# Splitting every gate and up piece of the short expert queues, with ScalarE evicting their up and the last turn inside the products before it

## The chip, the cores and the metric

The kernel runs on one core of a Trainium2 chip. The metric is the device time of one execution in microseconds. The core has five engines with a queue each, which meet in semaphores: TensorE (PE in the rows, its weight loads PEld), VectorE (DVE), ScalarE (ACT), GpSimd (POOL) and SyncE (SP), which issues the transfers from HBM.

## What is computed

A decoder trunk of two layers on 256 tokens of 1024 channels in float32. Each layer has a token mixer and then a channel mixer: in layer 0 a dense SwiGLU, in layer 1 a top-2-of-8 expert SwiGLU with 3584 inner channels. The change touches the expert part alone:

```python
def swiglu(h, wg, wu, wd):
    return (jax.nn.silu(h @ wg) * (h @ wu)) @ wd

def moe_swiglu(h2, router, wg, wu, wd):       # h2: 256 x 1024
    logits = jnp.matmul(h2, router, preferred_element_type=jnp.float32)
    top_logit, top_e = lax.top_k(logits, TOP_K)        # 2 of 8
    top_w = jax.nn.softmax(top_logit, axis=-1)
    ...
    # every token goes through its two experts; the results are added by weight
    yb = lax.map(expert_block, ...)                    # swiglu(xb, wg[e], wu[e], wd[e])
    return jnp.zeros_like(h2).at[tok_buf].add(yb * w_buf[:, None], mode='drop')
```

## The kernel before

From about 608 us on the kernel runs eight queues of tokens, one for each expert. Queues 0 to 3 are long (up to 128 tokens), queues 4 to 7 short (`SHORT = 64`); which expert stands in which queue is settled at run time by the number of its tokens. Each queue goes through its expert's 3584 inner channels in chunks of 512 (`CH`), two chunks in a step where possible: `steps` lists (queue, first channel, number m of chunks). A short queue has four steps, three with m = 2 and one with m = 1. After a start with two long steps, short and long steps take turns; the last two steps are short.

A step computes the gate product, then the up product (8 row blocks of 128 rows each, 512 columns a chunk), and then `down(*prev, ...)`: the down product of the step before. Weights come as raw tiles of 2 MB each and are used in pieces of 128 x 1024. float32 is computed in parts: `split` makes of a piece a high part `wh` (ScalarE, L121) and a low part `wl` (VectorE, L124). For a long queue the tokens are split too, and a product of 512 columns is three matmuls (L133 to L135). For a short queue the 64 tokens' high and low parts stand side by side as 128 columns of one operand (`xa` for gate and up, `ax` for down), and a product is two matmuls, with `wh` (L904) and `wl` (L905). Some pieces of short queues are not split: `piece(view, whole)` returns the raw view, and `products` multiplies it as float32 with an unsplit copy of the 64 tokens (`xw`, `aw`; L900). In the profile each such product is two matmul instructions. Whole are one gate piece of each short step (p = 1), one up piece of each short step with m = 2, and one of four down pieces.

`take` keeps as many pieces ready as there are buffers (`len(pieces)`, five pairs of wh and wl), so the splits of the next pieces stand in ScalarE's and VectorE's queues ahead of what the program does after taking a piece. `keep_order` fixes the order on PE, DVE and ACT as the code records it.

A short step's gate and up results are evicted from PSUM to SBUF: the gate as it is by ScalarE (L1257), the up by VectorE (L1261). The `turn` of a step happens during the next step's gate pieces: for a short queue TensorE multiplies gate and up rows with `fold` (L917), which turns them and adds the two halves, ScalarE takes Silu (L918), VectorE multiplies (L919), and both split the result into `ax` (L128, L129). For a long queue it is four transposes a half (L928), then L128 and L129 into `ax` and `al`. `dispatch` gathers the tokens of a queue (L828 and what follows), and `combine` brings a queue's result back to the tokens (L948 to L955); these are generators that `advance` moves a stage further at fixed pieces. The last step has no next step: behind the loop stand `settle()`, then its `turn`, and then its four down pieces with two products each.

Of the kernel before, what the change touches and what calls it, by code (L numbers as in the profile page):

```python
# [10 lines left out]
F32 = mybir.dt.float32  # L11
F32R = mybir.dt.float32r
# [3 lines left out]
AF = mybir.ActivationFunctionType  # L16
# [6 lines left out]
DB = D // 128  # L23
# [10 lines left out]
NLONG, SHORT, LEAD = 3, 64, 2  # L34
# [25 lines left out]
def trunk_kernel(ctx: ExitStack, tc: tile.TileContext, x, positions, norm1_g, w_in, q_norm_g, w_uq,  # L60
# [15 lines left out]
    consts = pool("consts", "left")  # L76
# [686 lines left out]
    def moe(l, norm, lgT):  # L763
        i = l // 2
        mp = pool("moe", "left")
# [54 lines left out]
        def is_short(r):  # L820
            return r > NLONG
# [9 lines left out]
        def dispatch(r):  # L831


            sh = is_short(r)
            if sh:
                xa = norm_pool.tile([128, DB, 128], F32R, name="xa", tag="hlo0")
                xw = mp.tile([128, 4, SHORT], F32, name="xw", tag="xw")
            else:
                xgh, xgl = (consts.tile([128, DB, 128], F32R, name="xg", tag=f"xT{k}") for k in range(2))
            io = iota2 if sh else iota  # L840
            P = mp.tile([128, 2, 128], BF16, name="P", tag="P", bufs=2)
            C = norm_pool.tile([128, 2, 128], F32, name="C", tag="nsq", bufs=2)
            for t in range(2):
                V.tensor_scalar(P[:, t], io, pos_r[:, t, r:r + 1], None, op0=OP.is_equal)
                V.tensor_scalar(C[:, t], io, pos_r[:, t, r:r + 1], wsel_r[:, t, r:r + 1], op0=OP.is_equal, op1=OP.mult)
            yield
            for j0 in range(0, DB, 4):
                pg = bank()
                gather(pg, j0, P)
                v = pg.rearrange("p (j s) -> p j s", j=4)  # L850
                js = slice(j0, j0 + 4)
                if sh:
                    if j0 == 0:
                        A.activation(xw, v[:, :, :SHORT], AF.Copy)
                    A.activation(xa[:, js, :SHORT], v[:, :, :SHORT], AF.Copy)
                    V.tensor_sub(xa[:, js, SHORT:], v[:, :, SHORT:], f32(xa[:, js, :SHORT]))
                else:
                    split_act(xgh[:, js], xgl[:, js], v)
            yield
            xg[r] = (xa, xw) if sh else (xgh, xgl)  # L860
            back[r] = places(C, sh)

        xg, back, expert = {}, {}, {}
# [9 lines left out]
        def wide(w_, r, f0, n):  # L873

            for h in range(n):
                w = raw_tile().rearrange("p (a b) -> p a b", a=DB // n)
                SP.dma_start(w, weights(w_, r, GU, FE, h * 512, D // n, f0, n * CH))
                a = 2 // n
                for p in range(4):
                    yield piece(w[:, p * a:(p + 1) * a], is_short(r) and h == 0 and p == 1 and (n == 2 or w_ is moe_w_gate))  # L880

        def deep(r, f0, n, by_block=False):

# [8 lines left out]
        def piece(view, whole):  # L892

            return (view,) if whole else split(view)

        def products(o, l, k, r, a, c, start, stop):


            if len(r) == 1:
                PE.matmul(o[:SHORT], l[1][:, k], r[0][:, a, c], start=start, stop=stop)  # L900
            elif l[0].shape[2] == l[1].shape[2]:
                mm3(o, (l[0][:, k], l[1][:, k]), (r[0][:, a, c], r[1][:, a, c]), start, stop)
            else:
                PE.matmul(o, l[0][:, k], r[0][:, a, c], start=start, stop=False)  # L904
                PE.matmul(o, l[0][:, k], r[1][:, a, c], start=False, stop=stop)  # L905

        def turn(r, s, h, acts, P=None):


            pt = bank()  # L910
            js = slice(4 * h, 4 * h + 4)
            if is_short(r):
                ax, aw = acts
                p4 = pt.rearrange("p (k b q) -> p k b q", k=2, b=4)
                for k in range(2):
                    for b in range(4):
                        PE.matmul(p4[:, k, b], s[k][:, (4 * h + b) * 128:(4 * h + b + 1) * 128], fold, start=True, stop=True)  # L917
                A.activation(aw[:, js], p4[:, 0], AF.Silu)  # L918
                V.tensor_mul(aw[:, js], aw[:, js], p4[:, 1])  # L919
                split_act(ax[:, js, :SHORT], ax[:, js, SHORT:], aw[:, js])  # L920
                return
            for b in range(4):
                c = slice(b * 128, (b + 1) * 128)
                if P is not None:
                    for t in range(2):
                        PE.matmul(pt[:, c], s[t][:, c], P[:, t], start=t == 0, stop=t == 1)
                else:
                    PE.transpose(pt[:, c], s[:, (4 * h + b) * 128:(4 * h + b + 1) * 128], ident)  # L928
            split_act(acts[0][:, js], acts[1][:, js], pt.rearrange("p (b q) -> p b q", b=4))
# [34 lines left out]
        def advance(tag="u", always=False):  # L964
            if behind and (always or met[0] - behind[0][1] >= len(pieces)):
                g = behind.pop(0)[0]
                aux[0] = tag
                if next(g, "end") != "end":
                    behind.insert(0, (g, met[0]))
                aux[0] = "u"  # L970
# [206 lines left out]
        def acts_of(r):  # L1177
            one = norm_pool.tile([128, DB, 128], F32R, name="ax", tag="hlo1")
            if is_short(r):
                return one, mp.tile([128, DB, SHORT], F32, name="aw", tag="al")  # L1180
            return one, mp.tile([128, DB, 128], F32R, name="al", tag="al")
# [28 lines left out]

        y = {}

        def down(r, f0, m, acts, banks_at):
            sh = is_short(r)
            if f0 == 0:
                if sh in pending:
                    settle()
                y[sh] = [bank(f"y{int(sh)}") for _ in range(2)]
            for p in range(4 * m):
                pc = take()  # L1220
                for n in range(2):
                    products(y[sh][n], acts, p, pc, 0, slice(n * 512, (n + 1) * 512), f0 == 0 and p == 0,
                             f0 + m * CH == FE and p == 4 * m - 1)
                if p in banks_at:
                    advance(banks_at[p])
            if f0 + m * CH == FE:
                pending.add(sh)
                begin(combine(y[sh], *back[r], sh))
# [3 lines left out]
        for r, f0, m in steps[1:]:  # L1232
            sh = is_short(r)
            while r not in back:
                advance(always=True)
            x = xg[r]
            acts = acts_of(prev[0])
            pg = [bank("g") for _ in range(m)]
            for w in range(2):
                if w:  # L1240
                    pu = [bank() for _ in range(m)]
                    u = rows_tile(1) if sh else None
                for p in range(4 * m):
                    pc = take()
                    for a in range(2 // m):
                        for n in range(m):
                            k = p if m == 2 else 2 * p + a
                            products((pu if w else pg)[n], x, k, pc, a, slice(n * CH, (n + 1) * CH), k == 0, k == DB - 1)
                    t = p - 2 * (m - 1)
                    if w == 0 and 0 <= t < prev[2]:  # L1250
                        turn(prev[0], last[0], t, acts, last[1])
                    elif w == 1 and m == 2 and p == 5:
                        advance("g")
                if w == 0:
                    s = rows_tile(0)
                    for n in range(m):
                        A.activation(s[:, n * CH:(n + 1) * CH], pg[n], AF.Copy if sh else AF.Silu)  # L1257
            for n in range(m):
                c = slice(n * CH, (n + 1) * CH)
                if sh:  # L1260
                    V.tensor_copy(u[:, c], pu[n])  # L1261
                else:
                    V.tensor_mul(s[:, c], s[:, c], pu[n])
            if f0 + m * CH == FE:
                after = r + 1 if r not in (NLONG, NE - 1) else None
                if after:
                    begin(dispatch(after))
            down(*prev, acts, {1: "g", 4: "u"} if m == 1 else {2: "g"} if prev[2] == 1 else {3: "g", 4: "u"})
            prev, last = (r, f0, m), ((s, u) if sh else s, None)

        settle()
        r, f0, m = prev
        acts = acts_of(r)
        turn(r, last[0], 0, acts)
        pcs = [take() for _ in range(4)]
        for n in range(2):
            for b, pc in enumerate(pcs):
# [56 lines left out]
```

## Time and profile before

| | |
|---|---|
| median of 3 runs | 1522.5 us (1522.24 to 1522.84) |
| the profiled execution | 1522.75 us, its span 1521.0 us |
| PE busy | 1487.3 us (98%) |
| PEld busy | 1229.0 us (81%) |
| DVE busy | 1266.6 us (83%) |
| ACT busy | 1017.9 us (67%) |
| POOL busy | 110.4 us (7%) |
| moved by the DMA queues | 439.69 MB, 289 GB/s over the span |

The profile is of one execution. A matmul is drawn from its start to a modelled end, and the next one starts before that end, so the pace of TensorE is read from one start to the next and not from lengths. Merged rows of a timeline (x11) give the first start and the time to the end of the last. "idle before <-releaser" is the time in which the engine stood, and whose semaphore ended it. PEclk is the granted clock of TensorE: 1.00 is 2.4 GHz, 0.50 is 1.2 GHz.

### The profile page before, as it was taken

How to read it: one execution, taken by the hardware profiler on the slowest of the kernel's cores; microseconds unless marked ns; L12 is line 12 of the kernel's file. 1: busy time of each engine (PE TensorE's matmuls, PEld its weight loads, DVE VectorE, ACT ScalarE, POOL GpSimd, SP SyncE). 2: the span in 40 equal slices, each digit the busy share in tenths (PEclk: the TensorE clock that was granted, in tenths of full speed). 3: DMA queues.
4: the chain of work that ended last, by engine and by line, in shares of the span. 5: the costliest groups of instructions: out<-in, count | busy, mean ns of one | idle time of the engine just before them, and what ended most of it. 6: DMA issues, size and time to landing. Idle time of an engine off the chain costs nothing.

```text
span 1521.0 us, 22641 instructions
## 1 busy us (share of the span) xinstructions
PE 1487.3 (98%) x8624; PEld 1229.0 (81%) x8624; DVE 1266.6 (83%) x1787; ACT 1017.9 (67%) x1319; POOL 110.4 (7%) x133
## 2 busy tenths in 40 slices
PE   6999999999999999999999999999999999999997
PEld 5899999999889988768677786777776777777764
DVE  6987876667887888988888998899898889898985
ACT  4596454444487466777776877686777677677773
POOL 5211400002211120000000000000000000000000
PEclk8999999999999999999999999999999999999998
DMA  7338645442336838999999999999999999999990
GB/s 229 112 111 330 224 151 202 148 130 96 115 108 250 304 125 313 381 362 406 358 390 359 351 389 368 374 396 370 346 394 356 387 385 371 350 395 348 405 345 29
DMA packets 139700, 439.69 MB, mean 289 GB/s; under 512 B 5934, under 2 KB 12180, under 8 KB 139588
## 3 DMA queue, kind: packets, MB, share of 16 engines
q1 hardware_dynamic: 139284, 437.58, 76.2%
q8 instruction: 69, 1.13, 0.3%
q0 software_dynamic: 272, 0.62, 0.2%
q14 instruction: 43, 0.35, 0.1%
q10 hardware_dynamic: 32, 0.01, 0.0%
HBM read 437.15 MB, written 1.05 MB: 288 GB/s over the span
## 4 chain that ended last, share of the span: by engine, by line
PE 90%; DVE 6%; ACT 1%; POOL 1%; issue 1%; DMA 1%; SPq 0%; DVEq 0%; ACTq 0%; POOLq 0%
PE bk L133 19%; PE bk L134 19%; PE bk L135 19%; PE bk L904 9%; PE bk L905 8%; PE bk L900 6%; PE bk L917 3%; DVE wl L124 2%; PE bk L828 1%; PE bk L928 1%; POOL nacc L307 1%; PE bk L517 1%; PE bk L540 1%; DMA raw<-in_w_in_dram 1%; PE bk L954 0%
## 5 line engine op out<-in xcount | busy, mean ns | idle before, releaser
L124 DVE TENSOR_TENSOR wl<-raw,wh 128x1024 fp32r<-128x1024 f32 x757 | 896.0, 1227 | 103.9 <-ACT wh L121 100.6
L121 ACT ACTIVATE wh<-raw 128x1024 fp32r<-128x1024 f32 x773 | 789.4, 1054 | 273.7 <-PE bk L134 141.5
L133 PE MATMUL bk<-hh,wh 128*128 128x256 f32 x800 | 233.0, 292 | 5.3 <-ACT hh L299 5.2
L134 PE MATMUL bk<-hlo,wh 128*128 128x256 f32 x800 | 228.9, 286 | 2.1 <-DVE hlo L300 2.1
L135 PE MATMUL bk<-hh,wl 128*128 128x256 f32 x800 | 227.7, 285 | 0.3 <-DVE wl L124 0.3
L133 PE MATMUL bk<-wh,xg 128*128 128x512 f32 x432 | 173.4, 401 | 0.0
L135 PE MATMUL bk<-wh,xg 128*128 128x512 f32 x432 | 170.7, 395 | 0.0
L134 PE MATMUL bk<-wl,xg 128*128 128x512 f32 x432 | 170.6, 395 | 0.0
L133 PEld LDWEIGHTS bk<-hh,wh 128*128 128x128 f32 x800 | 154.6, 194 | 7.5 <-ACT hh L299 5.5
L904 PE MATMUL bk<-wh,xa 128*128 128x512 f32 x392 | 158.6, 405 | 0.0
L134 PEld LDWEIGHTS bk<-hlo,wh 128*128 128x128 f32 x800 | 154.7, 193 | 4.1 <-DVE hlo L300 2.5
L135 PEld LDWEIGHTS bk<-hh,wl 128*128 128x128 f32 x800 | 154.4, 193 | 0.8 <-DVE wl L124 0.7
L905 PE MATMUL bk<-wl,xa 128*128 128x512 f32 x392 | 154.0, 393 | 0.0
L904 PEld LDWEIGHTS bk<-wh,xa 128*128 128x128 f32 x392 | 73.6, 188 | 34.0 <-ACT wh L121 13.0
L135 PEld LDWEIGHTS bk<-wh,xg 128*128 128x128 f32 x432 | 81.1, 188 | 19.5
L134 PEld LDWEIGHTS bk<-wl,xg 128*128 128x128 f32 x432 | 81.3, 188 | 18.1
L133 PEld LDWEIGHTS bk<-wh,xg 128*128 128x128 f32 x432 | 81.3, 188 | 18.1
L134 PE MATMUL bk<-wl,ax 128*128 128x512 f32 x224 | 88.9, 397 | 0.0
L133 PE MATMUL bk<-wh,ax 128*128 128x512 f32 x224 | 88.8, 397 | 0.0
L135 PE MATMUL bk<-wh,al 128*128 128x512 f32 x224 | 88.1, 393 | 0.0
L905 PEld LDWEIGHTS bk<-wl,xa 128*128 128x128 f32 x392 | 73.7, 188 | 14.8 <-DVE wl L124 0.2
L904 PE MATMUL bk<-wh,ax 128*128 128x512 f32 x170 | 71.4, 420 | 1.8 <-DVE ax L129 1.8
(351 smaller groups left out, 2263.4 us busy)
## 6 DMA issues: line engine op xcount, KB each, us to landing
raw<-in_moe_w_gate_dram SPq DMA_DIRECT2D x56, 2048.0 KB, 9.7
raw<-in_moe_w_up_dram SPq DMA_DIRECT2D x56, 2048.0 KB, 9.5
raw<-in_moe_w_down_dram SPq DMA_DIRECT2D x55, 2048.0 KB, 10.8
raw<-in_w_in_dram SPq DMA_DIRECT2D x12, 2048.0 KB, 7.7
raw<-in_ffn_w_gate_dram SPq DMA_DIRECT2D x5, 2048.0 KB, 9.1
raw<-in_ffn_w_up_dram SPq DMA_DIRECT2D x5, 2048.0 KB
raw<-in_ffn_w_down_dram SPq DMA_DIRECT2D x5, 2048.0 KB, 8.0
raw<-in_w_o_dram SPq DMA_DIRECT2D x4, 2048.0 KB
```

The source lines that it names most:

```text
L121: A.activation(hv, view, AF.Copy)
L124: eng.tensor_sub(lv, view, f32(hv))
L133: PE.matmul(o, l[0], r[0], start=start, stop=False, **kw)
L134: PE.matmul(o, l[0], r[1], start=False, stop=False, **kw)
L135: PE.matmul(o, l[1], r[0], start=False, stop=stop, **kw)
L307: G.tensor_add(self.acc, self.acc, sq)
L517: PE.matmul(ps[:, i], qT[:QD, h0 + i, t * 128:(t + 1) * 128], kT[:QD, h0 + i, :nk], start=True, stop=True)
L540: PE.matmul(po[:, i * VD:(i + 1) * VD], pTs[:, i * (t + 1) + kb], vt[:, kb, h0 + i], start=kb == 0, stop=kb == t)
L900: PE.matmul(o[:SHORT], l[1][:, k], r[0][:, a, c], start=start, stop=stop)
L904: PE.matmul(o, l[0][:, k], r[0][:, a, c], start=start, stop=False)
L905: PE.matmul(o, l[0][:, k], r[1][:, a, c], start=False, stop=stop)
L917: PE.matmul(p4[:, k, b], s[k][:, (4 * h + b) * 128:(4 * h + b + 1) * 128], fold, start=True, stop=True)
```

## The change

Every gate and up piece goes through `split`; only down pieces can be whole. `xw` is gone, and a short queue's tokens are the tuple `(xa,)`; `products` tells the kinds apart by that. The up of a short step is evicted by ScalarE (`A.activation(..., AF.Copy)`) instead of VectorE. The last step's `turn` is handed to the last `down` of the loop as `then`, which calls it after the products of the last piece but one; for this the operands of the last down products get places of their own (`ends`), in the memory of `xa` and of a long queue's tokens, which are free by then.

```diff
@@ dispatch
             if sh:
                 xa = norm_pool.tile([128, DB, 128], F32R, name="xa", tag="hlo0")
-                xw = mp.tile([128, 4, SHORT], F32, name="xw", tag="xw")
@@
                 if sh:
-                    if j0 == 0:
-                        A.activation(xw, v[:, :, :SHORT], AF.Copy)
                     A.activation(xa[:, js, :SHORT], v[:, :, :SHORT], AF.Copy)
@@
-            xg[r] = (xa, xw) if sh else (xgh, xgl)
+            xg[r] = (xa,) if sh else (xgh, xgl)
@@ wide
-                    yield piece(w[:, p * a:(p + 1) * a], is_short(r) and h == 0 and p == 1 and (n == 2 or w_ is moe_w_gate))
+                    yield split(w[:, p * a:(p + 1) * a])
@@ products
-            elif l[0].shape[2] == l[1].shape[2]:
+            elif len(l) == 2 and l[1].shape[2] == 128:
@@ down
-        def down(r, f0, m, acts, banks_at):
+        def down(r, f0, m, acts, banks_at, then=None):
@@
                 if p in banks_at:
                     advance(banks_at[p])
+                if then and p == 4 * m - 2:
+                    then()
@@ the loop over steps
                 if sh:
-                    V.tensor_copy(u[:, c], pu[n])
+                    A.activation(u[:, c], pu[n], AF.Copy)
@@
-            down(*prev, acts, {1: "g", 4: "u"} if m == 1 else {2: "g"} if prev[2] == 1 else {3: "g", 4: "u"})
+            then = None
+            if (r, f0, m) == steps[-1]:
+                ends = (norm_pool.tile([128, DB, 128], F32R, name="ax", tag="hlo0"),
+                        consts.tile([128, DB, SHORT], F32, name="aw", tag="xT0"))
+
+                def then():
+                    turn(r, (s, u), 0, ends)
+
+            down(*prev, acts, {1: "g", 4: "u"} if m == 1 else {2: "g"} if prev[2] == 1 else {3: "g", 4: "u"}, then)
@@ behind the loop
         settle()
         r, f0, m = prev
-        acts = acts_of(r)
-        turn(r, last[0], 0, acts)
+        acts = ends
         pcs = [take() for _ in range(4)]
```

The first place is VectorE in a short step of two chunks in the middle of the stage. `wl` is a split, `al` the second half of a long queue's turn, `s` the eviction of up (its tile shares a name with the gate's), `aw` the product in the next, short turn. The order before:

```order
L124 TENSOR_TENSOR wl<-raw,wh 128x1024 x9
L129 TENSOR_TENSOR al<-bk,ax 128x512
L124 TENSOR_TENSOR wl<-raw,wh 128x1024
L129 TENSOR_TENSOR al<-bk,ax 128x512
L124 TENSOR_TENSOR wl<-raw,wh 128x1024 x11
L1261 COPY s<-bk 128x512 x2
L124 TENSOR_TENSOR wl<-raw,wh 128x1024 x9
L919 TENSOR_TENSOR aw<-aw,bk 128x256
```

The same place in the changed kernel, whose line numbers are three lower here:

```order
L124 TENSOR_TENSOR wl<-raw,wh 128x1024 x10
L129 TENSOR_TENSOR al<-bk,ax 128x512
L124 TENSOR_TENSOR wl<-raw,wh 128x1024
L129 TENSOR_TENSOR al<-bk,ax 128x512
L124 TENSOR_TENSOR wl<-raw,wh 128x1024 x21
L916 TENSOR_TENSOR aw<-aw,bk 128x256
```

One split more stands ahead of the turn and one more behind it, and the two evictions between the splits are gone.

The second place is VectorE at the end of the program. `yl` and `xk` belong to the combines (`xk` is the sum over tokens), `aw` and `ax` to the last turn. Before:

```order
L955 TENSOR_TENSOR xk<-xk,bk 128x512 x2
L949 SCALAR_TENSOR_TENSOR yl<-bk,wp,yh 128x512
L124 TENSOR_TENSOR wl<-raw,wh 128x1024 x6
L955 TENSOR_TENSOR xk<-xk,bk 128x512 x2
L919 TENSOR_TENSOR aw<-aw,bk 128x256
L129 TENSOR_TENSOR ax<-aw,ax 128x4x64
L949 SCALAR_TENSOR_TENSOR yl<-bk,wp,yh 128x512
```

In the changed kernel:

```order
L952 TENSOR_TENSOR xk<-xk,bk 128x512 x2
L946 SCALAR_TENSOR_TENSOR yl<-bk,wp,yh 128x512
L124 TENSOR_TENSOR wl<-raw,wh 128x1024 x5
L916 TENSOR_TENSOR aw<-aw,bk 128x256
L129 TENSOR_TENSOR ax<-aw,ax 128x4x64
L124 TENSOR_TENSOR wl<-raw,wh 128x1024
L952 TENSOR_TENSOR xk<-xk,bk 128x512 x2
```

The last turn's two operations moved ahead of the last split and of the additions of the combine before. On TensorE the turn's eight products (16 matmul instructions) now stand ahead of the last piece of the down before it and ahead of that combine's four matmuls.

## Rows read from the trace of the kernel before

**Rows 1.** Stretches: busy us (count) by engine, PEclk, DMA share, GB/s.

```profile
600.00:1500.00 900.00, 898.59 (x4107) 668.58 (x4106) 800.00 (x819) 666.47 (x754) 0.00 (x0) 1.00 0.95 365
1400.00:1450.00 50.00, 50.00 (x221) 36.81 (x220) 44.23 (x44) 36.92 (x43) 0.00 (x0) 1.00 1.01 390
```

**Rows 2.** Waits, 600 to 1500 us: us in total, times, longest.

```profile
ACT wh L121 <- PE bk L135: 65.0, 188, 1.3
...
PEld bk L134 <- DVE wl L124: 1.3, 3, 0.4
...
PEld bk L905 <- DVE wl L124: 0.7, 2, 0.5
```

**Rows 3.** Timeline of PE around a whole piece: start us, us, operation.

```profile
1162.53 0.40 PE L905 MATMUL bk<-wl,xa 128*128 128x512 f32 x1
1162.86 1.93 PE L900 MATMUL bk<-raw,xw 128*64 128x512 f32 x4
...
1165.05 0.39 PE L905 MATMUL bk<-wl,xa 128*128 128x512 f32 x1
```

**Rows 4.** Groups by line and shape: busy us, mean ns | idle before.

```profile
L124 DVE TENSOR_TENSOR wl<-raw,wh 128x1024 fp32r<-128x1024 f32 x753 | 892.6, 1229 | 103.9 <-ACT wh L121 100.6
L121 ACT ACTIVATE wh<-raw 128x1024 fp32r<-128x1024 f32 x769 | 786.9, 1057 | 269.9 <-PE bk L134 139.3 <-PE bk L135 72.9 <-PE bk L904 35.8
...
L900 PE MATMUL bk<-raw,xw 128*64 128x512 f32 x112 | 54.1, 605 | 0.0
...
L1257 ACT ACTIVATE s<-bk 128x512 f32<-128x512 f32 x55 | 29.8, 589 | 0.0
...
L955 DVE TENSOR_TENSOR xk<-xk,bk 128x512 f32<-128x512 f32 x32 | 20.5, 682 | 5.2 <-PE bk L954 5.2
```

**Rows 5.** Timeline of DVE in the same short step.

```profile
1161.96 3.50 DVE L124 TENSOR_TENSOR wl<-raw,wh 128x1024 fp32r<-128x1024 f32 x3 [1.32 <-ACT wh L121]
1167.00 0.69 DVE L129 TENSOR_TENSOR al<-bk,ax 128x512 fp32r<-128x512 f32 x1 [1.54 <-ACT ax L128]
...
1169.09 0.69 DVE L129 TENSOR_TENSOR al<-bk,ax 128x512 fp32r<-128x512 f32 x1
1169.69 12.67 DVE L124 TENSOR_TENSOR wl<-raw,wh 128x1024 fp32r<-128x1024 f32 x11
1182.28 1.28 DVE L1261 COPY s<-bk 128x512 f32<-128x512 f32 x2
1183.48 10.30 DVE L124 TENSOR_TENSOR wl<-raw,wh 128x1024 fp32r<-128x1024 f32 x9
```

**Rows 6.** Timeline of PE in the same short step.

```profile
1167.10 0.60 PE L928 MATMUL bk<-ident,s 128*128 128x128 f32 x4
...
1167.77 0.39 PE L905 MATMUL bk<-wl,xa 128*128 128x512 f32 x1
...
1171.92 0.39 PE L905 MATMUL bk<-wl,xa 128*128 128x512 f32 x1
...
1179.05 0.39 PE L905 MATMUL bk<-wl,xa 128*128 128x512 f32 x1
...
1179.73 0.39 PE L133 MATMUL bk<-wh,ax 128*128 128x512 f32 x1
...
1181.12 0.40 PE L133 MATMUL bk<-wh,ax 128*128 128x512 f32 x1
```

**Rows 7.** Timeline of PE around the last turn.

```profile
1498.27 0.39 PE L954 MATMUL bk<-yl,PT 128*128 128x512 f32 x1
1500.40 2.00 PE L917 MATMUL bk<-fold,s 128*128 128x64 f32 x16 [1.74 <-DVE xk L955]
1504.23 0.79 PE L904 MATMUL bk<-wh,ax 128*128 128x512 f32 x1 [1.84 <-DVE ax L129]
...
1510.44 0.39 PE L905 MATMUL bk<-wl,ax 128*128 128x512 f32 x1
```

**Rows 8.** The stretch behind that turn, columns as in rows 1.

```profile
1504.20:1510.00 5.80, 5.77 (x14) 4.51 (x15) 0.75 (x1) 0.69 (x1) 0.00 (x0) 0.50 0.00 0
```

## The prediction

> **What bounds the kernel now.** I read the busy time by stage first. From 600 to 1500 us, the expert stage, TensorE is busy 898.59 of 900 us, VectorE 800.00 and ScalarE 666.47 [rows 1]. A busy TensorE could still hide pauses, because one matmul is drawn 0.39 us long and the next starts 0.23 us after it. So I next read the waits of that stage: TensorE's weight loads waited for a VectorE split five times, 2.0 us in all, while ScalarE waited 65.0 us in 188 waits for TensorE to give its piece buffers back [rows 2]. TensorE sets the pace, and the two splitting engines run up to five buffers ahead and then stand still. VectorE has 100 us of idle time in 900, so it is the next limit, and in short stretches it may already be the first.
>
> **A whole piece on TensorE.** Between the L905 ahead of one and the second L905 behind it [rows 3] lies all that it costs. Between the L905 at 1162.53 and the L905 at 1165.05 lie 2.52 us. Two of the intervals in it are ordinary. The 18 intervals from the L905 at 1167.77 to the one at 1171.92 [rows 6] give 4.15 / 18 = 0.2306 us, so the whole piece took 2.52 - 2 x 0.23 = 2.06 us, changing to the other kind of matmul and back included. Split, the same piece is two products of a high and a low part, 4 x 0.2306 = 0.92 us. The change turns 16 gate pieces (one for each short step) and 12 up pieces (one for each short step of two chunks) into split ones: 112 / 4 = 28 pieces [rows 4]. TensorE loses 28 x (2.06 - 0.92) = **31.9 us** of work.
>
> **The same pieces on ScalarE and VectorE.** A split costs VectorE 1.144 us when subtractions follow each other ((12.67 - 1.23) / 10 [rows 5]), and ScalarE 1.06 at most [rows 4]. So VectorE gets 28 x 1.144 = 32.0 us more, and gives 28 evictions of up away. Two in a row take 1.20, from the first at 1182.28 to the next subtraction at 1183.48 [rows 5], so 28 x 0.60 = 16.8 us less and 15.2 more in all. ScalarE gets 28 x 1.06 and 28 evictions of 0.589 at most [rows 4], 46 us, and loses four small copies into xw. That leaves it at some 711 of 890 us, and the time comes out of waits like the 65.0 us above: I cost ScalarE at nothing, and if that cover were gone, it would be 0.5 to 0.6 us for each eviction that VectorE's next split waits for.
>
> **Where VectorE becomes the late one.** TensorE takes 0.92 us for a split piece of a short queue, VectorE 1.144. A short step of two chunks has 16 such pieces in a row, then 8 pieces of a long queue, which last 1181.12 - 1179.73 = 1.39 us each [rows 6], so that VectorE catches up. The whole pieces were rests for VectorE within the run of 16. I follow one step by hand. The anchor is the second group of transposes, at 1167.10 [rows 6]; the second al follows at 1169.09, and from 1169.69 VectorE subtracts without a pause [rows 5]. In the order this run is x11: seven pieces of up (the whole one needs none) and four of the next down.
> Before: the last up piece is the seventh, done at 1169.69 + 6 x 1.144 + 1.23 = 1177.78. TensorE wants it at 1179.05 [rows 6], 1.27 us later.
> After: it is the eighth, done at 1178.93. TensorE wants it 1.14 us earlier, at 1167.77 + 44 x 0.2306 = 1177.92. It waits for 1.06 us with a start of 0.05 us. The first piece of down, done 1.144 us later, is wanted 0.92 us later: 0.22 us more. The second comes in time, for a down piece gives VectorE 1.39 us. Together 1.28 us.
> The anchor itself moves too. The gate's piece that was whole is now split ahead of the first al, and TensorE gets there 1.14 us earlier: VectorE is late by up to 2.28 us against it, and its waits in front of the al operations, 1.54 us in the row shown [rows 5], take up most. Remaining lateness lies between 0 and 1.1 us; I take 0.1, near the lower end, because the same step has a wait of 1.32 us just ahead. So 1.4 us a step, bounds 0.8 and 2.0 (the lower one if VectorE comes to the run half a split ahead of now, the upper with two thirds of that lateness; all of it is a rival below): 12 steps, **+16.8 us**.
> In three of these steps (the first ones of short queues 2 to 4) the combine of the queue before falls among the down pieces: two additions and a subtraction of 512 columns, three times about 0.60 (0.682 for an addition [rows 4], and 1.20 for two copies that follow each other). Between the second and the third down piece VectorE then needs 1.80 + 1.14, TensorE 1.39: 1.55, less the 0.25 that VectorE gained on the piece before, is 1.3, bounds 0 and 1.6, three times, **+3.9 us**. The four short steps of one chunk have half as many pieces, and only the last, which is not followed by a long queue, waits longer: **+0.8 us**, bounds 0 and 1.5.
>
> **The eviction of up.** It stands behind four splits on ScalarE, as the gate's already does, and those splits and the eviction are released by the same products. What is queued behind it, the fifth split, waits two evictions (about 1.0 us) longer; VectorE is then at least two pieces behind ScalarE, so nobody waits. VectorE's gain of 1.2 us there lets it catch up sooner.
>
> **The tail.** Now the last product ahead of the last turn starts at 1498.27, the first one behind it at 1504.23 [rows 7]: 5.73 us after 0.23 for the former, of which the turn's 16 matmuls need some 1.87. 3.86 us is idle: 1.74 for a bank that VectorE's addition frees, the rest for the turn's chain over ScalarE and VectorE. In the changed order the turn has the last piece of the down before and four matmuls of a combine behind it, 0.92 + 0.92 us, about the 1.84 us that TensorE now waits for the chain; I leave 0.3 us. And behind the pause the granted clock was 0.50, 1.2 GHz [rows 8]: from 1504.23 to 1510.44 lie 15 intervals, 6.21 us instead of 15 x 0.2306 = 3.46. That is 2.75. Together 3.86 - 0.3 + 2.75 = **6.3 us** less. The last 7 us (combine, store) stay.
>
> **Sum.** -31.9 + 16.8 + 3.9 + 0.8 - 6.3 = -16.7 us. The profiled execution took 1522.75 us, a span of 1521.0 and 1.75 around it that nothing here touches, so 1506.05; it lies 0.25 above the median of the runs, and I say **1505.8**.
>
> **Rivals.** *VectorE eats it nearly whole.* If the anchor's lateness is at its upper end, a step waits for 2.4 us: 12 x 2.42 + 4.7 = 33.7, and -31.9 + 33.7 - 6.3 = -4.5 leaves 1518. For it: the first half of VectorE's extra work lies ahead of the anchor. Against: its idle time there.
> *VectorE never binds.* Then 31.9 + 6.3 come off: 1484.3. Against: 0.92 below 1.144, and only five buffers between.
> *The weights' transfers bind.* The stage moves 365 GB/s at a share of 0.95; in one stretch it was 390 at 1.01 [rows 1]. The forecast shortens the 900 us by 31.9 - 21.5 = 10.4 and needs 365 x 900 / 889.6 = 369 on average, under the 384 to 386 that both rows give for a share of 1 (365 / 0.95, 390 / 1.01). For it: the share is near 1 already. If 365 were all there is, the body would keep its time and the tail's 6.3 us be left: 1516.2. The Trainium skill, "DMA: Bandwidth & Descriptors", section Specifications, lists 358 GB/s for a core's HBM and 368 as a vendor's derate: both rows here lie above the first, and by the second an estimate is 900 x (1 - 365 / 368) = 7 us for the body and 1509 in all.
> *The clock falls (slower).* The new waits are pauses of about 0.2 us, one a piece, seven or so in a short step. If the granted clock dropped in each of these 12 steps as it did in the tail, at 2.75 us each, it would be +33: 1522.5 - 16.7 + 33 = 1538.8. It decides from the seventh such step on (16.7 / 2.75 = 6.1). Against: in the tail TensorE had stood for 1.74 and 1.84 us with only 64-column matmuls between [rows 7], and through the 900 us with five short waits the clock stayed at 1.00 [rows 1, 2]. The Trainium skill's "TensorE: Matmul & The Clock Gate", section "A second HAM failure mode: psum-queue depth-cycling", says that frequent micro-idles between groups of matmuls made the clock oscillate in one kernel; by that rule this rival is the outcome, and no row here has such pauses to test it.
>
> **Chances.** Forecast with its bounds 0.80; VectorE eats it 0.05; VectorE never binds 0.05; transfers bind 0.06; the clock falls 0.04. The bounds of the steps give 12 x 0.6 = 7 us either way, so 1498.5 to 1512.5, and 1499 to 1513 is the range, with 0.2 left out. A measurement of this kernel can tell 0.2% (3 us) from no change. All cases but the last are faster by more; some of the first two rivals may shrink to nothing: faster 0.92, same 0.04, slower 0.04.
>
> **What would show it.** No matmul from raw and xw; in the second half of up TensorE starts a piece every 1.14 us, and its loads wait for wl in all 12 short steps of two chunks, about 20 us in all; VectorE's busy time in the stage up by about 15 us, ScalarE's by 44; clock 1.00 to the end, no pause ahead of the last turn. Wrong if those waits are under 10 or over 30 us, if a split waits for a transfer, or if the clock is below 1 between 620 and 1480.

## The result

The changed kernel takes 1508.4 us, the median of four runs (1506.96 to 1510.56), where the kernel before took 1522.7 beside it: a ratio of 0.9904 with a 95% interval of 0.9884 to 0.9923. Forecast were 1505.8 us and a range of 1499 to 1513. The profiled execution took 1506.96 us, its span 1505.1; forecast for that execution were 1506.05. So the median lies 2.6 us above its forecast and the profiled execution 0.9; the four runs spread over 3.6.

The clearest measure is the stretch from the first matmul on `xa` to the last matmul of the program. The rows below are the start and the end of it in the timeline of TensorE, of the kernel before and then of the changed one (start us, length us, operation):

```profile
607.74 0.40 PE L904 MATMUL bk<-wh,xa 128*128 128x512 f32 x1
...
1513.90 0.40 PE L954 MATMUL bk<-yl,PT 128*128 128x512 f32 x1
```

```profile
607.25 0.40 PE L901 MATMUL bk<-wh,xa 128*128 128x512 f32 x1
...
1498.28 0.40 PE L951 MATMUL bk<-yl,PT 128*128 128x512 f32 x1
```

That is 906.16 us before and 891.03 after, 15.13 less. The rest of the 15.79 between the two profiled executions is 0.49 ahead of the stretch and 0.17 behind it and around the span. In a second profile of the changed kernel (below, e1_same) the same two matmuls start at 609.35 and 1500.43: 891.08 us. So the stretch repeats to 0.1 us, while its start moves by 2 us from one execution to the next. "The stretch" always means this one from here on, and times of it, from profiles, tell the kernels apart better than medians do.

The stretch 600 to 1485 us of the changed kernel, columns as in rows 1:

```profile
600.00:1485.00 885.00, 880.87 (x4091) 668.11 (x4090) 804.77 (x813) 697.23 (x804) 0.00 (x0) 1.00 0.96 371
```

Against the 900 us of the first of rows 1, VectorE is 4.8 us busier in 15 us less, ScalarE 30.8, and the clock stands at 1.00. The transfers ran at 371 GB/s. The waits of that stretch, to be read against rows 2 (us in total, times, longest):

```profile
ACT wh L121 <- PE bk L135: 54.8, 158, 1.3
...
DVE wl L124 <- ACT wh L121: 39.1, 94, 1.3
PEld bk L902 <- DVE wl L124: 30.8, 79, 1.1
...
PEld bk L901 <- ACT wh L121: 17.9, 22, 0.8
...
PEld bk L134 <- DVE wl L124: 8.5, 18, 1.2
```

Where TensorE's loads waited five times for VectorE, they now wait 97 times. TensorE's row `PEld bk L901 <- ACT wh` has a counterpart in the kernel before (600 to 1500 us), which the prediction passes over:

```profile
PEld bk L904 <- ACT wh L121: 30.8, 38, 0.8
```

Each of these 38 and 22 waits stands directly behind a whole piece and is 0.81 us long, whenever ScalarE's split ended. They belong to the price of a whole piece and are no lateness of ScalarE. How the waits for VectorE look in one short step is shown by the timeline of TensorE in the second short step, which has the same order as the later one of rows 6: the first piece of gate, the second transposes, the first pieces of up, the last piece of up and the first of down.

```profile
671.63 0.39 PE L901 MATMUL bk<-wh,xa 128*128 128x512 f32 x1
...
675.73 0.60 PE L925 MATMUL bk<-ident,s 128*128 128x128 f32 x4
...
680.76 0.40 PE L901 MATMUL bk<-wh,xa 128*128 128x512 f32 x1
681.05 0.50 PE L902 MATMUL bk<-wl,xa 128*128 128x512 f32 x1
...
686.73 0.50 PE L902 MATMUL bk<-wl,xa 128*128 128x512 f32 x1
...
687.86 0.50 PE L902 MATMUL bk<-wl,xa 128*128 128x512 f32 x1
...
689.00 0.50 PE L134 MATMUL bk<-wl,ax 128*128 128x512 f32 x1
```

From the second up piece on the first product with `wl` starts late, and from one such start to the next are 1.13 us (686.73 to 687.86; 5.68 from 681.05 to 686.73 for five), VectorE's pace, not the 0.92 that TensorE needs. VectorE and then ScalarE in the same step, the answer to rows 5:

```profile
671.76 4.63 DVE L124 TENSOR_TENSOR wl<-raw,wh 128x1024 fp32r<-128x1024 f32 x4 [1.33 <-ACT wh L121]
676.31 0.68 DVE L129 TENSOR_TENSOR al<-bk,ax 128x512 fp32r<-128x512 f32 x1
676.91 1.22 DVE L124 TENSOR_TENSOR wl<-raw,wh 128x1024 fp32r<-128x1024 f32 x1
678.04 0.68 DVE L129 TENSOR_TENSOR al<-bk,ax 128x512 fp32r<-128x512 f32 x1
678.65 23.92 DVE L124 TENSOR_TENSOR wl<-raw,wh 128x1024 fp32r<-128x1024 f32 x21
```

```profile
676.91 3.90 ACT L121 ACTIVATE wh<-raw 128x1024 fp32r<-128x1024 f32 x4
680.71 1.08 ACT L1256 ACTIVATE s<-bk 128x512 f32<-128x512 f32 x2
681.66 7.70 ACT L121 ACTIVATE wh<-raw 128x1024 fp32r<-128x1024 f32 x8
689.25 1.09 ACT L1260 ACTIVATE s<-bk 128x512 f32<-128x512 f32 x2
```

VectorE runs from 671.76 on without a pause. ScalarE has none either: eight splits in 7.70 us are 0.95 each ((7.70 - 1.05) / 7), and the two evictions of the gate at 680.71 take as long as one split. This second fact I had not weighed, and it decides three of the experiments (e3_actlow, e4_nolow, e4_nosplit).

The end of the program, the answer to rows 7 and 8:

```profile
1487.38 1.89 PE L914 MATMUL bk<-fold,s 128*128 128x64 f32 x16
1489.08 0.47 PE L901 MATMUL bk<-wh,ax 128*128 128x512 f32 x1
...
1490.78 0.40 PE L951 MATMUL bk<-yl,PT 128*128 128x512 f32 x1
1491.11 0.50 PE L901 MATMUL bk<-wh,ax 128*128 128x512 f32 x1
...
1494.81 0.40 PE L902 MATMUL bk<-wl,ax 128*128 128x512 f32 x1
```

No pause stands ahead of the turn, and one of 0.1 us behind it where the last products begin. The 15 intervals from 1491.11 to 1494.81 take 3.70 us, where those of rows 7 took 6.21, and the granted clock is 1.00, where it was 0.50 in rows 8 (columns as there):

```profile
1490.00:1495.00 5.00, 5.00 (x22) 3.64 (x21) 3.74 (x6) 2.06 (x3) 0.00 (x0) 1.00 0.03 7
```

### The profile page after: what moved, and what is told of

Same layout as the page of the kernel before. It is cut to its first block, busy times and chain, and to the rows that moved or that the text cites. A ratio compares the mean times of both kernels' runs of the same rounds, so it can differ in the third digit from the quotient of the medians.

```text
span 1505.1 us, 22757 instructions
## 1 busy us (share of the span) xinstructions
PE 1471.6 (98%) x8624; PEld 1229.1 (82%) x8624; DVE 1276.8 (85%) x1787; ACT 1051.9 (70%) x1371; POOL 110.4 (7%) x133
## 3 DMA queue, kind: packets, MB, share of 16 engines
HBM read 437.15 MB, written 1.05 MB: 291 GB/s over the span
## 4 chain that ended last, share of the span: by engine, by line
PE 87%; DVE 8%; ACT 2%; issue 1%; POOL 1%; DMA 1%; SPq 0%; DVEq 0%; ACTq 0%; POOLq 0%
PE bk L134 19%; PE bk L133 19%; PE bk L135 19%; PE bk L902 9%; PE bk L901 8%; DVE wl L124 4%; PE bk L897 3%; PE bk L914 3%; PE bk L828 1%; ACT wh L121 1%; POOL nacc L307 1%; PE bk L517 1%; PE bk L540 1%; PE bk L925 1%; DMA raw<-in_w_in_dram 1%
## 5 line engine op out<-in xcount | busy, mean ns | idle before, releaser
L124 DVE TENSOR_TENSOR wl<-raw,wh 128x1024 fp32r<-128x1024 f32 x785 | 925.4, 1224 | 99.7 <-ACT wh L121 97.0
L121 ACT ACTIVATE wh<-raw 128x1024 fp32r<-128x1024 f32 x801 | 814.1, 1057 | 267.9 <-PE bk L134 141.5
L902 PE MATMUL bk<-wl,xa 128*128 128x512 f32 x448 | 184.2, 411 | 1.7 <-DVE wl L124 1.7
L901 PE MATMUL bk<-wh,xa 128*128 128x512 f32 x448 | 178.8, 399 | 0.1
L902 PEld LDWEIGHTS bk<-wl,xa 128*128 128x128 f32 x448 | 84.1, 188 | 45.4 <-DVE wl L124 30.3
L901 PEld LDWEIGHTS bk<-wh,xa 128*128 128x128 f32 x448 | 84.3, 188 | 14.5 <-PE bk L902 0.5
L901 PE MATMUL bk<-wh,ax 128*128 128x512 f32 x170 | 69.8, 411 | 0.0
```

The lines of the kernel that those rows point to most:

```text
L121: A.activation(hv, view, AF.Copy)
L124: eng.tensor_sub(lv, view, f32(hv))
```

## The experiments

All kernels of one group ran on one chip beside the kernel before. "Changed" is the changed kernel.

| kernel | median us | ratio to before, 95% | stretch us |
|---|---|---|---|
| before | 1523.0 to 1523.8 | 1 | 906.16 |
| changed again (e1_same) | 1508.0 | 0.9895, 0.988 to 0.991 | 891.08 |
| two raw tiles fewer a step (e1_half) | 1507.1 | 0.9891, 0.9876 to 0.9906 | 891.03 |
| one subtraction on GpSimd (e1_pool_up1) | 1522.3 | 0.999, 0.9981 to 0.9999 | 903.77 |
| second up piece whole (e1_upwhole) | 1499.2 | 0.9849, 0.9835 to 0.9862 | 883.46 |
| fourth up piece whole (e3_upwhole4th) | 1503.4 | 0.9864, 0.9848 to 0.988 | 887.63 |
| gate piece whole (e2_gatewhole) | 1519.9 | 0.9978, 0.9967 to 0.9989 | 902.03 |
| up evicted by VectorE (e2_dve) | 1513.2 | 0.994, 0.9921 to 0.9959 | 896.33 |
| before, new last turn (e2_tail) | 1517.8 | 0.9964, 0.9949 to 0.998 | 899.77 |
| changed, old last turn (e2_notail) | 1512.8 | 0.9936, 0.9919 to 0.9953 | 896.86 |
| copy on ScalarE for a subtraction (e3_actlow) | 1513.1 | 0.9927, 0.9911 to 0.9944 | 896.13 |
| one subtraction fewer (e4_nolow) | 1501.3 | 0.9853, 0.9835 to 0.987 | 884.77 |
| one split fewer (e4_nosplit) | 1496.2 | 0.9814, 0.9793 to 0.9835 | 877.37 |

### Is it the transfers, and where is the spread from?

> The changed kernel again, as the measure for the runs beside it. Four runs gave 1506.96 to 1510.56 us, a spread of 3.6 where the kernel before had 0.6. If the spread belongs to the kernel (weights that arrive late in some runs), it comes again; if not, the runs lie within 1 us of each other. Median expected 1507 to 1509.

> Leaves out the second raw tile of gate and of up in each short step of two chunks (24 transfers of 2 MB, some 50 MB of the stage's 325) and splits and multiplies the first tile twice, so the result lacks that part of the weights. Theory (VectorE's splits are what TensorE waits for): the time stays within 2 us of the changed kernel, and the waits for wl stay at some 1.2 us in each of 12 steps. Rival (transfers make the splits late): up to 14 us faster, waits gone. If transfers cause the spread between runs, the spread falls under 1 us here.

The second kernel loads the second raw tile of gate and up in a short step only `if h == 0`:

```diff
-                w = raw_tile().rearrange("p (a b) -> p a b", a=DB // n)
-                SP.dma_start(w, weights(w_, r, GU, FE, h * 512, D // n, f0, n * CH))
+                if h == 0 or not is_short(r):
+                    w = raw_tile().rearrange("p (a b) -> p a b", a=DB // n)
+                    SP.dma_start(w, weights(w_, r, GU, FE, h * 512, D // n, f0, n * CH))
```

With about 50 MB less to load the stretch is 891.03 us, as with all of it, so transfers hold nothing there. The runs lay 3.1 us apart with fewer transfers and 3.0 with all of them, and those of the kernel before 3.9, once there are 15 of them (1521.63 to 1525.53): the 0.6 us of its first three runs was chance. In the profiles of all these kernels the stretch starts between 606.70 and 611.17, although their code ahead of it differs little (the small copy into `xw`, the first splits and transfers of the stage). What moves the part ahead was not followed further.

### Is VectorE the late one?

> Of the changed kernel only the up piece goes back to whole (12 pieces); gate all split, ScalarE's eviction and the new place of the last turn stay. Theory: TensorE gets 12 x 1.14 = 13.7 us of work back and loses the waits that stand behind the up run, 12 x 1.2 to 1.4 and three combines at 0.8 to 1.3: 14.4 to 17 and 2.4 to 3.9, so 0.7 to 7 us faster than the changed kernel, 1501 to 1507. Rival (waits are not VectorE's): 13.7 slower, 1521.

```diff
-                    yield split(w[:, p * a:(p + 1) * a])
+                    yield piece(w[:, p * a:(p + 1) * a], is_short(r) and h == 0 and p == 1 and n == 2 and w_ is moe_w_up)
```

(and `xw` back, with its copy and its case in `products`.) The stretch is 7.6 us shorter than that of the changed kernel, just outside the 0.7 to 7 expected, and **this version beats both kernels**: 1499.2 us, with an interval that lies clear below that of the changed kernel. A typical short step, from the first matmul on `xa` to the first on `xg`, shows it: 29.06 us before (672.47 to 701.52), 28.40 changed (671.63 to 700.03), 27.88 here (670.59 to 698.47). The 1.14 us that a split gate piece gives come through in full there (29.06 - 27.88 = 1.18), and splitting the up piece on top gives away 0.52. It is so in eight of the nine ordinary steps of two chunks (1.14 to 1.21); the first of them gains 0.85, and the three with a combine 0.54 to 0.57, as TensorE waits about 0.8 us for VectorE in them here too. Of the 7.6 us, 3.9 come from the nine steps, 2.9 from the three and 0.8 from the last step.

> One subtraction of each short step of two chunks (the second up piece) goes from VectorE to GpSimd, which stands idle in the stage. Theory (VectorE falls behind TensorE by 0.22 us a piece in the run of 16 short pieces): VectorE gets 1.14 us back ahead of the point where it is late, nearly all waits go, 12 x 1.2 to 12 x 1.4 us less, 1492 to 1495. Rival one (the waits come from something else, such as ScalarE at 0.95 us a split, or transfers): within 3 us of the changed kernel. Rival two (GpSimd's own subtraction, 2.50 us elsewhere in the program, comes late or slows VectorE): up to 12 x 1.36 = 16 us slower.

```diff
-                    yield split(w[:, p * a:(p + 1) * a])
+                    yield split(w[:, p * a:(p + 1) * a], int(is_short(r) and n == 2 and w_ is moe_w_up and h == 0 and p == 1))
```

Rival two came: 12.7 us longer, more than the change had won on the splits. In the timeline of this kernel stand GpSimd's subtraction, the VectorE split that runs beside it, and TensorE's wait:

```profile
682.43 3.11 POOL L124 TENSOR_TENSOR wl<-raw,wh 128x1024 fp32r<-128x1024 f32 x1 [61.96 <-ACT wh L121]
```

```profile
683.33 3.29 DVE L124 TENSOR_TENSOR wl<-raw,wh 128x1024 fp32r<-128x1024 f32 x1
```

```profile
685.59 0.50 PE L902 MATMUL bk<-wl,xa 128*128 128x512 f32 x1 [1.00 <-POOL wl L124]
```

VectorE's split took 3.29 us instead of 1.22 and ended 1.08 after GpSimd's, about its own length, as if it had stood until GpSimd was done. In all 12 places it took 3.13 to 3.29. GpSimd thus cost VectorE 2.1 us to save it 1.14, and was late itself. So this run says nothing on what VectorE's work is worth, and VectorE's share had to be found in another way.

> The changed kernel, but in each of the 12 short steps of two chunks ScalarE writes a plain copy of the second up piece in the place of its low part, so that VectorE has one subtraction less and GpSimd none; that low part is wrong and this part of the computation left out. Theory (VectorE's lateness is all that TensorE waits for, and GpSimd's slow run was due to GpSimd): 12 x 1.14 us of waits go, 891.0 - 13.7 = 877, between 876 and 880 from the first matmul on xa to the last, 1493 to 1497 in all. Rival one (ScalarE, at 0.95 us a split and with two evictions in each run, is as near its end as VectorE, and one operation more makes it late): 883 to 892. Rival two (the order and not VectorE's amount of work is at fault, as the slow run with GpSimd would also allow): 890 and above.

```diff
+        if on_act:
+            A.activation(lv, view, AF.Copy)
+            return hv, lv
         n_split[0] += 1
```

(`on_act` is set for the second up piece of each short step of two chunks alone; that call is not in the excerpt.)

This fell out against my theory: 5.1 us longer, above even the range of the ScalarE rival and so, by the letter, in that of the order. The timeline of VectorE tells which it is:

```profile
680.99 1.22 DVE L127 TENSOR_TENSOR wl<-raw,wh 128x1024 fp32r<-128x1024 f32 x1
683.19 2.36 DVE L127 TENSOR_TENSOR wl<-raw,wh 128x1024 fp32r<-128x1024 f32 x2 [0.98 <-ACT wh L121]
686.06 14.85 DVE L127 TENSOR_TENSOR wl<-raw,wh 128x1024 fp32r<-128x1024 f32 x13 [0.51 <-ACT wh L121]
```

VectorE stands twice for ScalarE's high part: 0.98 us behind the extra copy, 0.51 behind the gate's evictions, 1.49 together and more than the 1.14 it was spared. By steps the loss is 0.53 to 0.69 us in the nine ordinary ones; the three with a combine lose nothing. The new theory was that ScalarE is only half a split ahead of VectorE in the changed kernel too, so that VectorE's work is worth about half its length, and that only a piece which spares both engines is worth the whole. Two kernels put it to the test.

> The changed kernel, but in each of the 12 short steps of two chunks the second up piece has no subtraction: its low part is that of the piece ahead (this leaves out part of the computation). VectorE has one split less, ScalarE as many as before, GpSimd none more. New theory (ScalarE is only about half a split ahead of VectorE there: in the run with the copy on ScalarE, VectorE stood for 0.98 us behind that copy and 0.51 behind the two evictions of the gate, and without the copy's 0.95 some 0.54 of it stay): 1.14 - 0.54 = 0.6 us a step, 12 x 0.6 = 7 us, 882 to 886 from the first matmul on xa to the last. Rival (VectorE alone is late): 891.0 - 13.7, 876 to 879. Second rival (ScalarE is the late one in the changed kernel): 890 to 891.

```diff
-                    yield split(w[:, p * a:(p + 1) * a])
+                    pc = split(w[:, p * a:(p + 1) * a], low=pc[1] if is_short(r) and h == 0 and p == 1 and n == 2 and w_ is moe_w_up else None)
+                    yield pc
```

(With `low`, `split` makes the high part alone and returns `low` beside it; those lines are not in the excerpt.)

> As the run beside it, but the second up piece is not split at all, and TensorE multiplies high and low part of the piece ahead once more (this leaves out part of the computation). TensorE has as many matmuls as in the changed kernel, ScalarE and VectorE one split less each. New theory (the two splitting engines are late together): all of 1.14 us a step comes off, 12 x 1.14 = 13.7, 876 to 879. Rival one (VectorE alone): the same as the run beside it to 1 us. Rival two (neither engine's amount of work, but the order, holds TensorE): both runs at 888 or above.

```diff
-                    yield split(w[:, p * a:(p + 1) * a])
+                    if not (is_short(r) and h == 0 and p == 1 and n == 2 and w_ is moe_w_up):
+                        pc = split(w[:, p * a:(p + 1) * a])
+                    yield pc
```

884.77 and 877.37 us: 6.3 and 13.7 less than the changed kernel, both inside the new theory's numbers and outside the rivals' numbers. In the first VectorE still stands for ScalarE, in the second it runs through (timeline of VectorE, first kernel and second):

```profile
681.90 3.61 DVE L128 TENSOR_TENSOR wl<-raw,wh 128x1024 fp32r<-128x1024 f32 x3
686.02 14.85 DVE L128 TENSOR_TENSOR wl<-raw,wh 128x1024 fp32r<-128x1024 f32 x13 [0.51 <-ACT wh L125]
```

```profile
680.94 19.38 DVE L124 TENSOR_TENSOR wl<-raw,wh 128x1024 fp32r<-128x1024 f32 x17
```

By steps, the subtraction alone is worth 0.23 to 0.42 us in nine steps and 1.02 to 1.04 in the three with a combine, and not 0.6 in each of twelve, so that its sum of 6.3 came near the expected 7 in part by luck; the whole split is worth 1.12 to 1.18 in all twelve.

What sets that worth can be read in the changed kernel: how far ScalarE is ahead of VectorE at the first split behind the gate's evictions. In the typical step ScalarE ends it at 682.73 and VectorE takes it at 683.18 (ScalarE, then VectorE):

```profile
681.66 1.07 ACT L121 ACTIVATE wh<-raw 128x1024 fp32r<-128x1024 f32 x1
```

```profile
683.18 1.22 DVE L124 TENSOR_TENSOR wl<-raw,wh 128x1024 fp32r<-128x1024 f32 x1
```

That lead is 0.45 us, and without the subtraction the step is 0.40 shorter. In the nine steps the lead is 0.29 to 0.45. In the three with a combine it is 1.06 to 1.07, because one operation of the combine (`yl`, 0.74 us) stands on VectorE ahead of the run. In each of the twelve steps the worth of the subtraction equals the lead to 0.1 us.

### Where a rest must stand

> As the version with the second up piece whole (883.5 us from the first matmul on xa to the last), but the fourth up piece is whole in its stead. Theory (a whole piece is a rest for VectorE that only helps what comes behind it; in the changed kernel TensorE loses 0.06 and then 0.2 us on each piece from the second on): the waits at the second and third piece, about 0.17 and 0.21 us, come back in 12 steps, 4 to 5 us, less up to 1.2 in the three steps with a combine, where the rest comes nearer to it: 886 to 888.5. Rival (only the number of whole pieces counts): 883 to 884.

```diff
-... h == 0 and p == 1 and n == 2 and w_ is moe_w_up
+... h == 0 and p == 3 and n == 2 and w_ is moe_w_up
```

887.63 us, in the range: as many whole pieces, 4.2 us longer than with the second piece whole, and still 3.4 shorter than the changed kernel. A whole piece spares the splitting engines what comes behind it; the waits of the pieces ahead of it are not given back. The steps with a combine lose 0.41 to 0.45 each, where less than in the others (0.19 to 0.42) was expected.

### The other parts one by one

> Of the changed kernel (1508.0 us beside the last runs, 891.0 us from the first matmul on xa to the last matmul) only the gate piece of each of 16 short steps goes back to whole; up stays split. Theory (the split gate piece is hidden: VectorE catches it up in its idle time ahead of the second transposes, the term of 0.1 us for the anchor): TensorE gets 16 x 1.0 to 1.14 us of work and no wait goes, 907 to 909 in that stretch and 1524 to 1526. Rival (the gate's extra split is carried into the run of up, up to 1.1 us a step): 12 x 1.1 us of waits go, 894 to 896 and 1511 to 1513.

```diff
-                    yield split(w[:, p * a:(p + 1) * a])
+                    yield piece(w[:, p * a:(p + 1) * a], is_short(r) and h == 0 and p == 1 and w_ is moe_w_gate)
```

(and `xw` back, as in e1_upwhole.) The stretch of 902.03 us lies between the theory and the rival: 11.0 us back instead of 16 to 18. Compared step by step with the changed kernel, a split gate piece is worth 0.82 us on average in nine steps of two chunks, 0.15 to 0.19 in the three with a combine, 1.02 to 1.09 in the first three steps of one chunk, nothing in the last one. So about 0.3 us of a gate piece comes back as lateness in an ordinary step, nearly all of it in the steps with a combine, and all of it in the last step. Beside e2_tail (899.77) this kernel, which has up split and ScalarE's eviction besides, is 2.3 us longer: splitting up without the gate loses.

> The changed kernel with the up evicted by VectorE again, as in the kernel before. Theory (ScalarE's eviction is free, and on VectorE it would stand 1.2 us among the down pieces, where VectorE has regained 0.25 us on each of three or four pieces): 0.2 to 0.5 us in each of 12 steps, and more in the three steps with a combine, so 2.4 to 8 us slower, 893 to 899 from the first matmul on xa to the last. Rival one (hidden either way): 891. Rival two (nothing regained, all 1.2 us paid 12 times and half of it in four steps): 908.

```diff
-                    A.activation(u[:, c], pu[n], AF.Copy)
+                    V.tensor_copy(u[:, c], pu[n])
```

896.33 us, 5.3 longer and in the range, but not where expected: 1.4 in the twelve steps of two chunks (five times 0.14 to 0.16, once 0.66), 1.4 in three steps of one chunk, 1.3 in two long steps, 1.2 at the end. Having ScalarE evict up is worth 5.3 us in the changed kernel.

> The kernel before with the new place of the last turn alone. Theory: the pause of 3.86 us goes but for 0.3, and the last 15 intervals run at full clock, 2.75 us: 6.3 us less, 899.9 in the stretch that took 906.2. Rival (the clock is low in the last products for another reason than the pause): 3.6 us less, 902.6.

> The changed kernel with the last turn where it was. Theory (the parts add up): 6.3 us slower than the changed kernel, 897.3 in the stretch that took 891.0. Rival (the changed kernel's splits reach the tail, so that the part is worth another amount there): outside 896.5 to 898.

```diff
+                if then and p == 4 * m - 2:
+                    then()
```

(This is the core of the edit in e2_tail; `then` and `ends` come with it as in the change, and e2_notail takes all of it out of the changed kernel.) The new place of the last turn takes 6.39 us off the kernel before (906.16 - 899.77), and 5.83 off the changed one (896.86 - 891.03). It adds up with the rest to 0.6 us. Both times lie where the theory put them (899.9 and 897.3), and not at the 902.6 of the rival whose clock stays low for another reason than the pause.

## Why the prediction came out as it did

The steps' lengths in the two profiles give each term. Each gate or up piece that is no longer whole counts as 1.14 us less.

| term | forecast | measured |
|---|---|---|
| nine steps of two chunks, waits each | 1.4 | 1.58 |
| three with a combine, waits each | 2.7 | 2.71 |
| first three steps of one chunk, each | -1.14 | -1.29 |
| last step of one chunk and tail | -6.6 | -6.25 |
| stretch | -16.7 | -15.13 |

(Waits are 2 x 1.14 less what the step became shorter: in the nine steps 0.33 to 0.93, 6.28 in all, so 9 x 2.28 - 6.28 = 14.24; the three became 1.28 longer, 6.84 + 1.28 = 8.12.)

**The whole pieces (-31.9): right.** In e1_upwhole, in the eight ordinary steps of two chunks where hardly anything waits, a split gate piece takes 1.14 to 1.21 us off. In the first three steps of one chunk it is 1.25 to 1.30.

**VectorE late in the run of 16 (+16.8): right in mechanism, a little small.** The term that was too small is the lateness of the anchor, which I took as 0.1 us. From the second transposes to the second `al` were 1.99 us before, from 1167.10 to 1169.09 [rows 5, 6], and are 2.31 now, from 675.73 to 678.04: 0.32. The kernel with the gate whole gives the same 0.3 of a gate piece. VectorE's 1.54 us of idle time did go, as assumed, but they were not quite enough. The nine steps' difference to the forecast, 1.6 us, is what the stretch is off; the steps of one chunk (0.45 better) and the end (0.4 worse) cancel.

**The combines (+3.9): right in place, and the near-exact sum is luck.** 2.71 stand against 1.4 + 1.3 forecast. By the starts of matmuls TensorE waits 1.02 to 1.04 us at the third down piece, behind the three operations of the combine, where 1.3 were forecast; 1.63 to 1.67 are lost in up instead of 1.4, since `yl` ahead of the run makes VectorE later there. **The last step of one chunk**: VectorE is late there from the second half of up on, 1.2 us instead of 0.8. It follows from the table's row: -6.25 + 6.33 + 1.14 = 1.2, with 6.33 for that stretch of e2_tail.

**ScalarE at nothing: right for the eviction, but not for the reason that I gave.** VectorE takes the first split behind the evictions of up 0.84 to 2.33 us after ScalarE has ended it, in every short step but the last, so it waits for none of them; in the typical step it is 0.99, which is less than the two pieces that I had assumed. I wrote that ScalarE has time left from its waits for TensorE. It has in the stage, but none within the run of a short step, where it works without a pause and is 0.29 to 0.45 us ahead of VectorE behind the gate's evictions. That this made no difference to the time is because VectorE was slower still; the same reasoning would have misjudged a change that spares VectorE alone, as e3_actlow and e4_nolow show.

**The tail (-6.3): right**, -6.4 alone and -5.8 with the rest.

**The rivals.** That VectorE eats nearly all or that it never binds is out by the steps' lengths. Transfers do not bind: e1_half. The Trainium skill's derate in "DMA: Bandwidth & Descriptors", section Specifications, 368 GB/s, does not hold here as a bound: the row of the stage has 371. The clock did not fall: the stage's row has 1.00 through the 97 waits. The Trainium skill's "TensorE: Matmul & The Clock Gate", section "A second HAM failure mode: psum-queue depth-cycling", made frequent micro-idles a reason for an oscillating clock; with pauses of 0.1 to 0.2 us at nearly every piece of a run, and some of 0.9, this trace does not agree.

**The signs.** A piece every 1.14 us: yes, but already from the second piece of up on. Loads waiting for `wl` about 20 us, wrong above 30: by that view it is 39.3 (30.8 + 8.5), so this sign says wrong although the steps lost 14.24 + 8.12 + 1.22 = 23.6 us against 21.5 forecast. In the rows of the typical step a load stands idle for 0.37 to 0.38 us at each piece, while the starts of matmuls lose 0.21: the load's idle time begins while TensorE still works on the matmul before. The sign should have been put in starts of matmuls. VectorE's busy time rose by 10.2 us over the whole run, not 15, and ScalarE's by 34.0, not 44. For ScalarE I had counted lengths that rows draw for one operation (1.06, 0.589) where in a run the pace counts (0.95 and some 0.48 here, 28 x 1.43 = 40); what is left of both differences was not followed. The other signs came: no matmul from `raw` and `xw`, a clock of 1.00 through the stage and in the last products, no pause ahead of the last turn, and no split that waits for a transfer.

What the forecast did not ask is whether the whole change is worth having. Its own working has the answer: a split up piece gains 1.14 us on TensorE and costs 1.144 on an engine that is already behind. The gate with ScalarE's eviction is worth 16.3 us (899.77 - 883.46), up on top loses 7.6.

## What to carry to other kernels

Where two engines prepare what a third uses, work taken off the later one was worth no more here than the lead that the other has over it; look at both in the stretch where the third waits, not at their busy shares of the stage. An unprepared piece that costs the bound engine more can still pay when it spares both others, and pays more the nearer it stands to the head of a run (here 7.6 us at the second of eight, 3.4 at the fourth). Split an edit that treats two places alike, here gate and up, and price each by what stands behind it.

## What the runs showed of the hardware

That GpSimd slows VectorE was a rival; that VectorE seems to stand still altogether was not expected. VectorE's split beside GpSimd's took 3.29 us and ended 1.08 after it, and GpSimd's own took 3.11 where it took 2.50 on average elsewhere; it had started while VectorE's split before it was still running. In the nine steps where that was so GpSimd's took 2.95 to 3.11; in the three with a combine it started beside an `al`, which has one operand in PSUM, and took 2.37 or 2.38. The Trainium skill, "SBUF — State Buffer", section "Who interferes with whom", says that a VectorE instruction with two inputs in SBUF contends with a GpSimd instruction that reads SBUF, through a shared port that is locked exclusively; these rows agree.

The stretch of 890 us repeated to 0.1 us between profiles of a kernel, while its start moved by up to 4.5 us between kernels whose code is nearly the same up to there.
